# A gated delta-rule chain beside dense projections: the chain's output products are given out one by one behind a projection's product

## The chip, the cores and the metric

One NeuronCore of a Trainium2 chip runs the whole program. The metric is the device time of one execution in microseconds (us); the time of a kernel is the median of its runs.

## The reference

One layer of a streaming encoder for 2048 prompt frames and 32 sample frames of width 1024: a wide input projection, then two branches on the same normalised rows (banded softmax attention, and a gated delta rule with 8 heads of width 64), each gated and projected, merged, projected again and layer-normalised. What matters here is the delta rule, which runs over blocks of 64 frames in order:

```
def step(s, blk_in):
    q_c, k_c, u_c, w_c, gc_c, qk_c = blk_in
    v_new = u_c - einsum('bhld,bhde->bhle', w_c, s)
    o_c = einsum(q_c * exp(gc_c), s) + einsum('bhij,bhje->bhie', qk_c, v_new)
    k_dec = k_c * exp(g_last - gc_c)
    s = s * exp(g_last) + einsum('bhld,bhle->bhde', k_dec, v_new)
    return s, o_c
s_final, o = lax.scan(step, s0, (qb, kb, u, w, gc, qk))
```

The state s of one step needs the one before it; the output o_c is needed by nothing in the scan.

## The kernel before

The prompt is worked in two halves of 1024 frames (the second also carries the 32 sample frames). In each half TensorE runs the input projection as jobs: a job multiplies one 128-column block of weights with all rows, and to keep precision with float16 operands it does so in three products, hi x whi, hi x wlo and lo x whi, of 128x512 or 128x272 (in the order: `pj<-hi,whi` and so on, each with its own weight load `LDWEIGHTS whi` or `LDWEIGHTS wlo`). Meanwhile the delta rule of the heads whose projections are done is prepared (`system`, `solve`, `inverse`, `side`) and then run (`chain`). After these, attention, the branch projections, the merge and the output projection follow, on the same engines.

Nothing here is ordered by a compiler. The code is a set of generators ("streams"). A small planner, `Flow`, keeps a clock for each stream and a busy time for each engine, runs the stream with the earliest clock until it yields, and records its instructions on their engines in that order. `Engine.price` is the planner's cost of an instruction, `Mark` an event that streams may wait for, `Gate` a count of buffers. The engines then run their own queues in the recorded order and wait for each other by semaphores. The helper that records every instruction has one line, L267, so most rows of the profile carry it.

`chain` is one stream in each half. Two heads (a head pair) lie on the 128 partitions as a block-diagonal operand. It runs units of one or two head pairs in turn: a *single* unit has one product of each kind in a step, a *joint* unit two ("lanes"). A half has a single unit, three joint units and a single unit of 8 steps each, and the second half two joint steps of the sample more. A step has these products, all 128x64 in float32:

- `x<-state,k_bd`: keys with the state; VectorE then makes `r`
- `x<-r,u_bd`: the solved system with r; VectorE then makes `vn`, the new values
- `o<-state,q_bd`: the first output product, into bank o, which starts the sum
- `x<-vn,kd_bd`: the state's increment; VectorE then makes the next `state` from it and `faded`, which GpSimd makes (`fade`)
- `o<-vn,qk_bd`: the second output product, which ends the sum in bank o; ScalarE then copies it to `v_t`

The four that read `x` or feed it are the chain; the two into `o` are the outputs. Before, `outputs` records its products at once, right behind those of u_bd and of kd_bd, and puts the stream's clock back so that the planner does not count them in the chain's own time:

```
t = flow.cur.clock
for i, m in enumerate(ms_):
    PE.matmul(os_[i], m, x[:, i], start=not last, stop=last)
flow.cur.clock = t
```

Of the kernel before, what the change touches and what calls it, by code (L numbers as in the profile page):

```python
# [11 lines left out]
F32 = mybir.dt.float32  # L12
# [32 lines left out]


NQK = 4

NPAR, NSIDE = 4, 3
HEAD, TAIL = [2, 3], [6, 5]  # L50
# [28 lines left out]
class Stream:  # L79
    def __init__(self, gen, clock):  # L80
        self.gen, self.clock, self.last = gen, clock, None
# [75 lines left out]
class Flow:  # L157
# [2 lines left out]


    def __init__(self):
        self.heap, self.n, self.busy = [], 0, {}
        self.cur = Stream(None, 0.0)

    def push(self, s, later=0.0):
# [27 lines left out]
    def spend(self, key, cost):  # L194
# [6 lines left out]
        self.busy[key] = s.clock = t  # L201
        s.last = key


    def transfer(self, queue, size):

        start = max(self.cur.clock + 0.2, self.busy.get(queue, 0.0)) + 0.5
        self.busy[queue] = start

        end = max(start + 0.6, self.busy.get("DMA", 0.0)) + size / 360e3  # L210
        self.busy["DMA"] = end
        return end + MARGIN
# [13 lines left out]
class Engine:  # L226
# [36 lines left out]
    def __getattr__(self, name):  # L263
        f = getattr(self.eng, name)

        def call(*a, **k):
            r = f(*a, **k)  # L267
            self.flow.spend(self.key, self.price(name, a, k))
            return r

        setattr(self, name, call)
        return call
# [3 lines left out]
def trunk(ctx: ExitStack, tc: tile.TileContext, x_p, x_s, cache_k, cache_v, st_conv, st_gdn,  # L276
# [4 lines left out]
    flow = Flow()  # L281
    V = Engine(flow, nc.vector, "V")
    S = Engine(flow, nc.scalar, "S")
    G = Engine(flow, nc.gpsimd, "G")
    PE = Engine(flow, nc.tensor, "PE")
# [22 lines left out]
    def gate(n):  # L308
        return Gate(flow, n)

    def places(n):
        return Places(flow, n)

    def mark():
        return Mark(flow)
# [15 lines left out]
    def pt(tag):  # L331

        return bank_pool[tag].tile([P, 512], F32, tag=tag, bufs=banks[tag], name=tag)
# [506 lines left out]
    def phase_b(half):  # L840
# [4 lines left out]
        last = half == 1  # L845
# [77 lines left out]

        raw_slots, qk_slots, v_slots = gate(2), gate(NQK), gate(2)
        par_slots, side_slots, u_slots, p_slots, vt_slots = (places(n) for n in (NPAR, NSIDE, NSIDE, NSIDE, NSIDE))
# [101 lines left out]
        def job_conv(p, i):  # L1027
# [11 lines left out]
            def finish(b):  # L1039
                k = blocks[p][b]  # L1040
                if i == 0:
                    yield qk_slots
                    k.qk = bp.tile([P, 2, 512], F32, tag="qk", bufs=NQK, name=f"qk{p}{b}")
                if i == 2:
# [336 lines left out]
        xb, ob_ = pt("x"), [pt("o")[:, 0:HD] for _ in range(2)]  # L1381
        left = [len(order)]

        def lanes(ap):
            return ap.rearrange("p (l d) -> p l d", d=HD)

        def outputs(ms_, x, os_, last):

            t = flow.cur.clock
            for i, m in enumerate(ms_):  # L1390
                PE.matmul(os_[i], m, x[:, i], start=not last, stop=last)
            flow.cur.clock = t

        def keep(os_, vcs, end):
            yield
            for i, vc in enumerate(vcs):
                S.copy(out=vc, in_=os_[i])
            for m in end:
                m.done()

        def fade(out, st, by, m):
            G.tensor_tensor(out=out, in0=st, in1=by, op=ALU.mult)
            m.done()
            yield

        def chain(units):
            for ks in units:
                for k in ks:
                    yield k.ready
                a = ks[0]  # L1410
                if a.p is None:
                    steps = [([(a, c), (a, c + 1)], a.sc[:, 1, c:c + 2], a.sc[:, 3, c:c + 2], state_s[:, c:c + 2])
                             for c in range(0, NP, 2)]
                else:
                    some = a.both[:, a.lane:a.lane + len(ks)]
                    steps = [([(k, c) for k in ks], some[:, :, 1, c], some[:, :, 3, c], state[:, a.p:a.p + len(ks)])
                             for c in range(8)]
                for n, (who, by, fading, st) in enumerate(steps):
                    m = len(who)
                    by, fading = (x.unsqueeze(2).to_broadcast([P, m, HD]) for x in (by, fading))  # L1420
                    xs, ys, ds_ = (lanes(xb[:, i * P:i * P + m * HD]) for i in range(3))
                    vcs = [k.v_t[:, c if k.p is None else c % 4 * 2 + c // 4, :] for k, c in who]
                    for i, (k, c) in enumerate(who):
                        PE.matmul(xs[:, i], k.kb[:, c, :], st[:, i], start=True, stop=True)
                    faded, kept = bp.tile([P, 2, HD], F32, tag="st", bufs=1, name="st")[:, 0:m], mark()
                    flow.start(fade(faded, st, fading, kept))
                    yield
                    r = bp.tile([P, 2, HD], F32, tag="r", bufs=1, name="r")
                    for i, (k, c) in enumerate(who):
                        V.scalar_tensor_tensor(out=r[:, i], in0=xs[:, i], scalar=k.negc[:, c:c + 1], in1=vcs[i],  # L1430
                                               op0=ALU.mult, op1=ALU.add)
                    yield
                    for i, (k, c) in enumerate(who):
                        PE.matmul(ys[:, i], k.ub[:, c, :], r[:, i], start=True, stop=True)
                    outputs([k.qb[:, c, :] for k, c in who], st, ob_, False)
                    yield
                    vn = bp.tile([P, 2, HD], F32, tag="vn", bufs=1, name="vn")[:, 0:m]
                    V.tensor_tensor(out=vn, in0=ys, in1=by, op=ALU.mult)
                    yield
                    for i, (k, c) in enumerate(who):  # L1440
                        PE.matmul(ds_[:, i], k.kdb[:, c, :], vn[:, i], start=True, stop=True)
                    outputs([k.qkb[:, c, :] for k, c in who], vn, ob_, True)
                    flow.start(keep(ob_, vcs, [k.out for k in ks] if n == len(steps) - 1 else ()),
                               flow.busy["PE"])
                    yield kept
                    yield
                    V.tensor_tensor(out=st, in0=faded, in1=ds_, op=ALU.add)
                    yield
                for k in ks:
                    yield k.out  # L1450
                for k in ks:
                    par_slots.back(k.par)
                    side_slots.back(k.sn)
                    u_slots.back(k.un)
                    flow.start(tail(k))
# [85 lines left out]
        for g in (zeros(), worker(todo), worker(decays), prep(), local(), solve(), solve()):  # L1541
            flow.start(g)
        flow.start(chain([order[0:1], order[1:3], order[3:5], order[5:7], order[7:8]] + [[sample]] * last))
        return stack, make, done

# [954 lines left out]
    for half in range(2):  # L2500
        stack, make, done = phase_b(half)
        enter(1, half, make)
        flow.run(done)
        stack.close()
        stack_w.close()
        if half:
            wr_pool.append(ctx.enter_context(tc.tile_pool(name="wr0", bufs=1)))
            wr_open.done()
            gp = ctx.enter_context(tc.tile_pool(name="gp", bufs=1, reuse_waits="tile"))
            for gen in (early_g(), early_sg(), early(), load_a(), merge()):  # L2510
                flow.start(gen)
        ap, stack, make, done = phase_a(half)
        enter(0, half, make)
        if half == 0:
            flow.start(build_h(1, ap, 4), flow.cur.clock + AHEAD)
        if half == 0:
            flow.run(done)
            flow.run(l_ready[1][8])
            stack.close()
        else:  # L2520
            for p in range(NP):
                dma(ng_p[2 * p:2 * p + 2].rearrange("h k v -> (h k) v"), state[:, p, :])
                dma(ng_s[2 * p:2 * p + 2].rearrange("h k v -> (h k) v"), state_s[:, p, :])
            flow.start(carries(), flow.cur.clock + 20.0)
            flow.run(done)
            stack.close()
# [53 lines left out]
```

## Time and profile before

| | |
|---|---|
| median of 3 runs | 1965.35 us (1964.91 to 1971.32) |
| the profiled execution | 1972.64 us |
| its span on the core | 1970.6 us |
| TensorE (PE) busy | 1905.6 us, 97% |
| VectorE (DVE) busy | 1397.4 us, 71% |
| ScalarE (ACT) busy | 993.9 us, 50% |
| GpSimd (POOL) busy | 806.9 us, 41% |
| mean granted clock of TensorE | 0.984 |

The span is the time from the first to the last instruction in the trace; the execution's own time has some 2 us around it. The profiled execution is one of the longer ones, 7.3 us over the median. PE is the matmuls, PEld the loads of their weights, which run beside them. Matmuls overlap each other in the records, so the durations of a row of them add up to more than the time that passes.

### The profile page before, as it was taken

How to read it: one execution, taken by the hardware profiler on the slowest of the kernel's cores; microseconds unless marked ns; L12 is line 12 of the kernel's file. 1: busy time of each engine (PE TensorE's matmuls, PEld its weight loads, DVE VectorE, ACT ScalarE, POOL GpSimd, SP SyncE). 2: the span in 40 equal slices, each digit the busy share in tenths (PEclk: the TensorE clock that was granted, in tenths of full speed). 3: DMA queues.
4: the chain of work that ended last, by engine and by line, in shares of the span. 5: the costliest groups of instructions: out<-in, count | busy, mean ns of one | idle time of the engine just before them, and what ended most of it. 6: DMA issues, size and time to landing. Idle time of an engine off the chain costs nothing. (4 is left out here: it accounts for less than half of the span.)

```text
span 1970.6 us, 40977 instructions
## 1 busy us (share of the span) xinstructions
PE 1905.6 (97%) x14514; PEld 1348.8 (68%) x14514; DVE 1397.4 (71%) x4252; ACT 993.9 (50%) x2022; POOL 806.9 (41%) x1161
## 2 busy tenths in 40 slices
PE   8999999999999998999999999999999999999998
PEld 5455676666455556666767768768877667988886
DVE  7689988963278768679987986455556565465797
ACT  6665545443587777565544443355356675321110
POOL 7345436424344345444434432422122232243673
PEclk8999999999999999999999998999999999999999
DMA  3234332333368787223232142477878688896552
GB/s 132 71 89 118 72 105 78 91 87 93 115 156 212 165 183 169 77 79 84 76 94 74 52 126 57 130 207 198 223 180 189 168 199 187 255 332 200 174 189 87
DMA packets 382949, 274.61 MB, mean 139 GB/s; under 512 B 248338, under 2 KB 319358, under 8 KB 382744
## 3 DMA queue, kind: packets, MB, share of 16 engines
q1 hardware_dynamic: 382744, 272.00, 51.3%
q8 instruction: 114, 1.87, 0.4%
q14 instruction: 91, 0.75, 0.1%
HBM read 157.15 MB, written 71.76 MB: 116 GB/s over the span
## 5 line engine op out<-in xcount | busy, mean ns | idle before, releaser
L267 PE MATMUL pj<-hi,whi 128*128 128x512 f16 (+2 forms) x1992 | 643.3, 339 | 13.8 <-ACT part L267 3.1
L267 PE MATMUL pj<-hi,wlo 128*128 128x512 f16 (+2 forms) x1952 | 634.1, 339 | 0.7 <-POOL wlo L267 0.7
L267 PEld LDWEIGHTS <-whi 128*128 128x128 f16 x3984 | 395.9, 101 | 247.5 <-issue 7.2
L267 POOL TENSOR_TENSOR wlo<-wraw,whi 128x256 f16<-128x256 f32 (+1 forms) x392 | 282.2, 742 | 375.2 <-ACT whi L267 308.9
L267 PE MATMUL pj<-lo,whi 128*128 128x512 f16 (+2 forms) x1992 | 435.7, 338 | 0.0
L267 PEld LDWEIGHTS <-wlo 128*128 128x128 f16 x1952 | 198.2, 102 | 130.2 <-issue 10.2
L267 ACT ACTIVATE sb<-sb,mx,unit 128x640 f32<-128x640 f32 (+4 forms) x128 | 108.8, 850 | 95.0 <-DVE mx L267 85.6
L267 POOL TENSOR_TENSOR pu<-sb,pu 128x640 f16<-128x640 f32 (+2 forms) x64 | 81.4, 1273 | 178.3 <-ACT pu L267 140.7
L267 ACT ACTIVATE wraw<-wraw,w_scale 128x1024 f32<-128x1024 f32 (+1 forms) x98 | 111.4, 1137 | 81.2 <-DVE w_scale L267 77.7
L267 ACT CAST whi<-wraw 128x512 f16<-128x512 f32 (+2 forms) x212 | 128.1, 610 | 23.8 <-PE pj L267 20.8
L267 DVE SCALAR_TENSOR_TENSOR acc<-raw,cwT,acc 128x512 f32<-128x512 f32 x144 | 114.0, 792 | 13.9 <-ACT acc L267 12.6
L267 ACT CAST mh<-sf 128x256 fp32r<-128x256 f32 x64 | 25.7, 406 | 159.1 <-PE c L267 78.2
L267 DVE CUSTOM_DVE_ANT_0 sb<-a,bias 128x320 f32<-128x320 f32 (+5 forms) x136 | 66.3, 497 | 48.7 <-PE a L267 43.3
L267 ACT ACTIVATE sig<-pj,w_both 128x512 f32<-128x512 f32 (+2 forms) x84 | 49.2, 586 | 93.9 <-PE pj L267 75.3
L267 DVE SCALAR_TENSOR_TENSOR sys_u<-sys_p,sys_u 128x20 f32<-128x20 f32 (+11 forms) x408 | 93.3, 271 | 1.2
L267 POOL TENSOR_TENSOR ml<-sf,mh 128x256 fp32r<-128x256 f32 x60 | 59.7, 997 | 79.1 <-PE c L267 53.1
L267 POOL TENSOR_TENSOR st<-state,sc 128x128 f32<-128x128 f32 (+1 forms) x80 | 31.1, 388 | 148.4 <-DVE state L267 129.4
L267 PE MATMUL b<-ghi,whi 128*128 128x256 f32 (+1 forms) x320 | 89.4, 312 | 0.1
L267 DVE TENSOR_TENSOR sys_t<-sys_u,sys_p 128x60 f32<-128x60 f32 (+17 forms) x323 | 81.9, 254 | 6.0
L267 DVE TENSOR_TENSOR sys_u<-sys_u,sys_t 128x60 f32<-128x60 f32 (+17 forms) x323 | 81.6, 253 | 6.0 <-DVE state L267 0.2
L267 POOL TENSOR_TENSOR w_scale<-w_scale,mhalf 128x1 f32<-128x1 f32 x49 | 32.5, 663 | 124.7 <-DVE w_scale L267 115.3
L267 ACT CAST pu<-sb 128x640 f16<-128x640 f32 (+4 forms) x128 | 81.7, 649 | 0.5
(390 smaller groups left out, 4197.2 us busy)
## 6 DMA issues: line engine op xcount, KB each, us to landing
wraw<-in_w_in SPq DMA_DIRECT2D x192, 256.0 KB
sf<-sig SPq DMA_DIRECT2D x112, 128.0 KB
sig<-sig SPq DMA_DIRECT2D x44, 256.0 KB
sg<-sig SPq DMA_DIRECT2D x37, 256.0 KB
sig<-sg SPq DMA_DIRECT2D x37, 256.0 KB
sys_p<-sol_p SPq DMA_DIRECT2D x68, 128.0 KB
x<-in_x_p SPq DMA_DIRECT2D x16, 512.0 KB
xt<-in_x_p SPq DMA_DIRECT2D x16, 512.0 KB
```

The costliest lines, as they stand in the source:

```text
L267: r = f(*a, **k)
```

## The change

The planner gets a flag, `flow.wide`: whether the last product recorded on TensorE has a float32 weight operand. A generator, `flow.apart()`, yields up to three times (`TRIES`) while the flag is set, each time until 0.05 us (`GAP`) behind TensorE's busy time, so that another stream may record a product first. In `chain` the first of each kind of product asks `apart` before it is recorded, and the second lane's follows at once. The outputs become a stream of their own, started 0.15 us behind TensorE's busy time, in which every product asks `apart`. Since they can now be recorded later than the step that made them, marks keep the order: `taken` (the copies out of bank o are recorded) before the next first output product, `first` (the first output products are recorded) before the second ones and before the state is overwritten. The copies out of bank o, a stream of their own before (`keep`), are recorded at the end of the same stream. The fade is started one yield later.

```
+TRIES, GAP = 3, 0.05
...
+    def apart(self):
+        for _ in range(TRIES):
+            if not self.wide:
+                return
+            yield max(self.cur.clock, self.busy["PE"]) + GAP
...
+            if self.key == "PE":
+                self.flow.wide = a[1].dtype == F32
...
-        def outputs(ms_, x, os_, last):
-            t = flow.cur.clock
+        def outputs(ms_, x, os_, go, gone, vcs=None, end=()):
+            yield go
             for i, m in enumerate(ms_):
-                PE.matmul(os_[i], m, x[:, i], start=not last, stop=last)
-            flow.cur.clock = t
-        def keep(os_, vcs, end):
-            yield
-            for i, vc in enumerate(vcs):
-                S.copy(out=vc, in_=os_[i])
-            for m in end:
-                m.done()
+                yield from flow.apart()
+                PE.matmul(os_[i], m, x[:, i], start=vcs is None, stop=vcs is not None)
+            if vcs is None:
+                gone.done()
+            yield
+            if vcs is not None:
+                for i, vc in enumerate(vcs):
+                    S.copy(out=vc, in_=os_[i])
+                gone.done()
+                for m in end:
+                    m.done()
...
                     for i, (k, c) in enumerate(who):
+                        if not i:
+                            yield from flow.apart()
                         PE.matmul(xs[:, i], k.kb[:, c, :], st[:, i], start=True, stop=True)
+                    first = mark()
+                    yield
...
-                    outputs([k.qb[:, c, :] for k, c in who], st, ob_, False)
+                    flow.start(outputs([k.qb[:, c, :] for k, c in who], st, ob_, taken, first), flow.busy["PE"] + 0.15)
...
-                    outputs([k.qkb[:, c, :] for k, c in who], vn, ob_, True)
-                    flow.start(keep(ob_, vcs, [k.out for k in ks] if n == len(steps) - 1 else ()),
-                               flow.busy["PE"])
+                    taken = mark()
+                    flow.start(outputs([k.qkb[:, c, :] for k, c in who], vn, ob_, first, taken, vcs,
+                                       [k.out for k in ks] if n == len(steps) - 1 else ()), flow.busy["PE"] + 0.15)
+                    yield
                     yield kept
+                    yield first
```

(The products with u_bd and kd_bd get the same two lines on `apart` as that with k_bd.)

What this does to the order of instructions, on TensorE in the first joint step of the first half, from the products with u_bd on (the numbers behind k_bd, u_bd, q_bd, kd_bd and qk_bd are buffers, one for each lane; a float32 product loads its weights itself and has no row for it). Before:

```order
L267 MATMUL x<-r,u_bd_748 128x64
L267 MATMUL x<-r,u_bd_749 128x64
L267 MATMUL o<-state,q_bd_742 128x64
L267 MATMUL o<-state,q_bd_743 128x64
L267 LDWEIGHTS whi
L267 MATMUL pj<-hi_164,whi 128x512
L267 LDWEIGHTS wlo
L267 MATMUL pj<-hi_164,wlo 128x512
```

The same place after:

```order
L275 MATMUL x<-r,u_bd_748 128x64
L275 MATMUL x<-r,u_bd_749 128x64
L275 LDWEIGHTS whi
L275 MATMUL pj<-hi_164,whi 128x512
L275 MATMUL o<-state,q_bd_742 128x64
L275 LDWEIGHTS wlo
L275 MATMUL pj<-hi_164,wlo 128x512
L275 MATMUL o<-state,q_bd_743 128x64
L275 LDWEIGHTS whi
L275 MATMUL pj<-hi_164,whi 128x512
```

Each of the two output products now has a projection's product in front of it and one behind it, where all four float32 products stood in a row.

The second place is the end of the same step on TensorE, from the products with kd_bd to the next step's with k_bd. Before:

```order
L267 MATMUL x<-vn,kd_bd_745 128x64
L267 MATMUL x<-vn,kd_bd_746 128x64
L267 MATMUL o<-vn,qk_bd_738 128x64
L267 MATMUL o<-vn,qk_bd_739 128x64
L267 LDWEIGHTS whi
L267 MATMUL pj<-hi_164,whi 128x512
L267 MATMUL x<-state,k_bd_734 128x64
L267 MATMUL x<-state,k_bd_735 128x64
```

After:

```order
L275 MATMUL x<-vn,kd_bd_745 128x64
L275 MATMUL x<-vn,kd_bd_746 128x64
L275 LDWEIGHTS wlo
L275 MATMUL pj<-hi_164,wlo 128x512
L275 MATMUL o<-vn,qk_bd_738 128x64
L275 LDWEIGHTS whi
L275 MATMUL pj<-hi_164,whi 128x512
L275 MATMUL o<-vn,qk_bd_739 128x64
L275 LDWEIGHTS wlo
L275 MATMUL pj<-hi_164,wlo 128x512
L275 MATMUL x<-state,k_bd_734 128x64
L275 MATMUL x<-state,k_bd_735 128x64
```

Here three projection products stand between kd_bd and the next k_bd, where there was one.

More of the change, by code (lines that the diff above doesn't have):

```diff
@@ L162, in __init__ @@
     def __init__(self):
-        self.heap, self.n, self.busy = [], 0, {}
+        self.heap, self.n, self.busy, self.wide = [], 0, {}, False
         self.cur = Stream(None, 0.0)
@@ L1406, in chain @@
         def chain(units):
+            taken = mark()
+            taken.done()
             for ks in units:
@@ L1433, in chain @@
                     for i, (k, c) in enumerate(who):
+                        if not i:
+                            yield from flow.apart()
                         PE.matmul(ys[:, i], k.ub[:, c, :], r[:, i], start=True, stop=True)
-                    outputs([k.qb[:, c, :] for k, c in who], st, ob_, False)
+                    flow.start(outputs([k.qb[:, c, :] for k, c in who], st, ob_, taken, first), flow.busy["PE"] + 0.15)
                     yield
@@ L1440, in chain @@
                     for i, (k, c) in enumerate(who):
+                        if not i:
+                            yield from flow.apart()
                         PE.matmul(ds_[:, i], k.kdb[:, c, :], vn[:, i], start=True, stop=True)
-                    outputs([k.qkb[:, c, :] for k, c in who], vn, ob_, True)
-                    flow.start(keep(ob_, vcs, [k.out for k in ks] if n == len(steps) - 1 else ()),
-                               flow.busy["PE"])
+                    taken = mark()
+                    flow.start(outputs([k.qkb[:, c, :] for k, c in who], vn, ob_, first, taken, vcs,
+                                       [k.out for k in ks] if n == len(steps) - 1 else ()), flow.busy["PE"] + 0.15)
+                    yield
                     yield kept
+                    yield first
                     yield
```

## The prediction

> **What bounds the kernel now.** I read the page first: the span, the busy shares, and the chain that ended last.
>
> ```profile
> span 1970.6 us, 40977 instructions
> PE 1905.6 (97%) x14514; PEld 1348.8 (68%) x14514; DVE 1397.4 (71%) x4252; ACT 993.9 (50%) x2022; POOL 806.9 (41%) x1161
> PE pj L267 3%; PE a L267 3%; PE b L267 2%; PE c L267 1%; DVE xt L267 0%; POOLq L2574 0%; DVE fst L267 0%; DVE sl L267 0%; DVE m L267 0%; DVEq L267 0%; POOLq L267 0%
> ```
>
> TensorE is busy 97% of the span and the chain consists of its products, so a shorter row of products on TensorE shortens the run. Busy is not peak: matmuls overlap in the records, so what a product costs has to be read from start to start. The second view is therefore the timeline of TensorE inside a joint step and a single step. Columns: start, time covered, engine, line, product, how many of them. A float32 product shows as two records, so x4 is one pair of lanes and x2 one lane.
>
> ```profile
> 360.19 0.38 PE L267 MATMUL pj<-hi,wlo 128*128 128x512 f16 x1
> 360.40 0.38 PE L267 MATMUL pj<-hi,whi 128*128 128x512 f16 x1
> 360.62 0.55 PE L267 MATMUL x<-vn,kd_bd 128*128 128x64 f32 x4
> 361.01 0.61 PE L267 MATMUL o<-vn,qk_bd 128*128 128x64 f32 x4
> 361.46 0.38 PE L267 MATMUL pj<-hi,wlo 128*128 128x512 f16 x1
> 361.67 0.55 PE L267 MATMUL x<-state,k_bd 128*128 128x64 f32 x4
> 362.06 0.38 PE L267 MATMUL pj<-hi,whi 128*128 128x512 f16 x1
> ...
> 459.06 0.33 PE L267 MATMUL x<-state,k_bd 128*128 128x64 f32 x2
> 459.23 0.38 PE L267 MATMUL pj<-hi,whi 128*128 128x512 f16 x1
> ...
> 460.05 0.39 PE L267 MATMUL o<-state,q_bd 128*128 128x64 f32 x2
> 460.27 0.38 PE L267 MATMUL pj<-hi,wlo 128*128 128x512 f16 x1
> ```
>
> A projection's product takes 0.21 to 0.22 us to the next start (360.19, 360.40, 360.62). The same pair of float32 products takes 0.39 us behind a projection's product (360.62 to 361.01; also 361.67 to 362.06) and 0.45 us behind other float32 products (361.01 to 361.46). One lane alone: 0.17 behind a projection's product (459.06 to 459.23), 0.22 behind float32 (460.05 to 460.27). So each float32 group that gets a projection's product in front of it saves 0.05 to 0.06 us, whether it holds one product or two. The projection's product behind the group pays nothing: 361.46 to 361.67 and 362.06 onward are the usual steps.
>
> The weight loads (PEld) show why:
>
> ```profile
> 354.97 0.63 PEld L267 LDWEIGHTS x<-vn,kd_bd 128*128 128x128 f32 x4
> 355.52 0.53 PEld L267 LDWEIGHTS o<-vn,qk_bd 128*128 128x128 f32 x4
> ...
> 355.18 0.55 PE L267 MATMUL x<-vn,kd_bd 128*128 128x64 f32 x4
> 355.57 0.61 PE L267 MATMUL o<-vn,qk_bd 128*128 128x64 f32 x4
> ```
>
> Behind a projection's product the first load starts 0.21 us ahead of its matmul (354.97 to 355.18), beside the 512 columns in flight. Behind a float32 product, it starts 0.05 us ahead (355.52 to 355.57): the product in front streams 64 columns and is over before the load is.
>
> **The change part by part.** *How many groups move.* The rows of the state tiles give the counts:
>
> ```profile
> L267 PE MATMUL o<-vn,qk_bd x264: 274/275/422, 196.5 to 1251.4; 128*128 128x64 f32 x132
> L267 PE MATMUL o<-state,q_bd x256: 274/275/421, 195.4 to 1243.2; 128*128 128x64 f32 x128
> L267 PE MATMUL o<-state_s,q_bd x8: 275/275/276, 1246.4 to 1250.4; 128*128 128x64 f32 x8
> L267 DVE TENSOR_TENSOR vn<-x,sc x82: 208/283/293, 196.0 to 1250.2; 128x128 f32<-128x128 f32 x50, 128x64 f32<-128x64 f32 x32
> ```
>
> There are 82 steps: 50 joint (two lanes) and 32 single, so 132 products of each of the two output kinds. In the order before, all 264 stand behind a float32 product. In the order after, I count 262 of them each behind a projection's product; two of the qk kind are left behind float32. Of the inner chain products, the first with u_bd goes from 78 to 82 such places and the first with kd_bd from 76 to 82; with k_bd it stays at 79. That is 262 + 4 + 6 = 272 groups. At 0.055 us (the middle of 0.05 and 0.06) this is **-15.0 us**; by the two ends -13.6 and -16.3. Step by step it is the same: a joint step's output products fall from 2 x 0.45 to 4 x 0.17, -0.22, times 50 = -11.0; a single step's from 2 x 0.22 to 2 x 0.17, -0.10, times 32 = -3.2; the ten inner groups add -0.6: -14.8 from rounded rows.
>
> The Trainium skill, TensorE: Matmul & The Clock Gate, section LDWEIGHTS (loading the stationary operand), prices a load at columns / 1.2 ns, whatever the element's width: about 107 ns for 128 columns. The trace puts 0.45 / 4 = 0.11 between float32 records, so they agree on what sets that pace; as an estimate, hiding a load of 107 ns where 56 ns were hidden would make the sum 272 x 0.051 = 13.9 us in place of 15.0.
>
> *The k_bd load.* In 271.15 to 272.69 below, k_bd has a projection's product in front and still takes 0.44, since its state was ready too late for the load to run ahead.
>
> ```profile
> 271.58 0.61 PE L267 MATMUL o<-vn,qk_bd 128*128 128x64 f32 x4
> 272.03 0.38 PE L267 MATMUL pj<-lo,whi 128*128 128x512 f16 x1
> 272.25 0.61 PE L267 MATMUL x<-state,k_bd 128*128 128x64 f32 x4
> 272.69 0.38 PE L267 MATMUL pj<-lo,whi 128*128 128x512 f16 x1
> ```
>
> In the order after, mostly more products stand between kd_bd and the next k_bd. If that helps, it is worth up to 0.05 for each such step, of which I count 16 in the timeline: 0 to -0.8. I take -0.4.
>
> *The early branch products.* Of their 512 triples, 40 more use bank b in place of pj. The first of a run costs more than the next:
>
> ```profile
> 1301.42 0.36 PE L267 MATMUL b<-ghi,whi 128*128 128x256 f32 x1
> 1301.62 0.28 PE L267 MATMUL b<-ghi,wlo 128*128 128x256 f32 x1
> 1301.73 0.28 PE L267 MATMUL b<-ghi,whi 128*128 128x256 f32 x1
> ```
>
> 0.20 against 0.11; nine more such runs start behind a projection's product, +0.8 if all are new, 0 if the runs are as many as before. I take +0.4.
>
> *New waits.* The output products with q_bd now wait for a mark that the last step's copies out of bank o set. Those copies were given out a whole step earlier, and so I cost the wait at nothing; if a copy is late, everything behind it on TensorE waits, by the longest such wait below. The state's update on VectorE now also needs the q_bd products to be done; in both orders shown they stand ahead of kd_bd, for which it waits anyway: nothing. ScalarE's copies out of o come later by the products put in between (some 0.4 to 0.8 us a step). ScalarE already stands 101.1 us there:
>
> ```profile
> ACT v_t L267 <- PE o L267: 101.1, 57, 5.0
> PEld x L267 <- DVE r L267: 14.0, 37, 2.4
> PE x L267 <- DVE r L267: 2.6, 3, 1.9
> ```
>
> Behind them on ScalarE are the splits of weights into whi and TensorE's bank evacuations; at 50% busy it has room. The fade on GpSimd moves behind k_bd's mark by nothing that the order shows. No DMA is added or removed; SP's queue keeps its kinds and amounts, shifted by some rows. I price the whole reshuffle at zero with an uncertainty: it moves waits, and a wait on TensorE can cost more than its length:
>
> ```profile
> 1018.52 0.38 PE L267 MATMUL pj<-hi,whi 128*128 128x512 f16 x1
> 1020.76 0.66 PE L267 MATMUL x<-r,u_bd 128*128 128x64 f32 x4 [1.86 <-DVE r L267]
> ...
> 1019.00:1022.10 3.10, 1.33 (x11) 1.20 (x11) 3.03 (x13) 0.58 (x3) 1.18 (x4) 1.00 0.12 20
> 1022.10:1028.90 6.80, 6.80 (x28) 5.24 (x28) 4.02 (x22) 0.65 (x3) 0.40 (x1) 0.50 0.41 107
> 1195.00:1199.50 4.50, 4.50 (x87) 3.96 (x87) 3.73 (x17) 0.87 (x3) 0.17 (x1) 1.00 0.02 4
> 1199.60:1209.80 10.20, 10.20 (x43) 8.25 (x42) 5.10 (x20) 4.00 (x10) 3.36 (x6) 0.50 0.12 41
> ```
>
> (Windows: stretch, its length, then PE, PEld, DVE, ACT, POOL busy, the granted clock, DMA share, GB/s.) After u_bd waited 2.0 us beyond a product's usual step, the clock was granted at 0.50 for 6.8 us, which costs half of it: 2.0 + 3.4 = 5.4 us. The stretch from 1199.6 costs 5.1 us, with TensorE busy all of the 4.50 us ahead of it.
>
> *Sum.* -15.0 - 0.4 + 0.4 = **-15.0 us**. The profiled execution took 1972.64 us around its span of 1970.6, so it becomes 1957.6. It lies 7.3 us above the median of the runs, 1965.35; against that median the forecast is **1950.4 us**, -0.76%. A measurement of this kernel tells about 0.3% from no change, 5.9 us.
>
> **The rivals.** *VectorE takes the gain back (about 1962).* Where chains start, VectorE is nearly full:
>
> ```profile
> 190.00:290.00 100.00, 96.79 (x799) 64.89 (x799) 94.18 (x358) 55.22 (x117) 44.83 (x80) 1.00 0.39 100
> 940.00:1010.00 70.00, 68.00 (x594) 50.94 (x593) 67.14 (x241) 37.90 (x82) 30.03 (x58) 1.00 0.29 76
> ```
>
> For: 94.18 of 100 and 67.14 of 70. Against: the first window holds 8 single and 8 joint steps, 8 x 0.10 + 8 x 0.22 = 2.6 us, and 100 - 2.6 is still over 94.18; the second holds 8 single steps, 0.8 us of the 2.9 that VectorE has free. Two new waits like that at 1018.74, 10.8 us, would leave -4.2: about 1961, no change to be told.
>
> *Slower.* The same mechanism, more often: TensorE reaches u_bd sooner after k_bd, r is not there, and the half clock follows. It decides from four such waits: 21.6 - 15.0 = +6.6; with five, 1965.35 + 12.0 = 1977. Against: the matmuls' waits on r come to 2.6 us in 3, with one that long (the weight loads' 14.0 in 37 lie mostly beside a product in flight), and the order has about as many products between k_bd and u_bd as before.
>
> *The half clock recedes (about 1942).* The stretch from 1199.6 follows busy time in which joint steps run, with float32 products that spend half of their 0.11 us on loads; the change takes them apart there and fills the array better. If it and the one at 1022.1 go, 5.1 + 3.4 = 8.5 us more: 1950.4 - 8.5 = 1941.9. Against: the next order can have its own. The page named above, Part 1, says the clock follows how busy TensorE has been in windows of 3.4 us; the lengths here, 6.8 and 10.2, are multiples of that, and the second stretch shows that idle time is not needed.
>
> *The place makes no difference (1965).* If loads were hidden behind whatever product is in front, nothing would be won. The 0.45 against 0.39 of the same shapes speak against it. The same page, Part 2, Step-by-step, has the next tile's weights load while this one's matmul runs, without a word on how long that matmul is; taken so, it is this rival, and the rows say otherwise.
>
> **How the numbers follow.** Forecast 0.65; half clock recedes 0.17; gain taken back by VectorE's waits or never there 0.12 (0.02 of it the last rival); slower 0.06. So faster 0.65 + 0.17 = 0.82, same 0.12, slower 0.06. The range has the receding half clock at its low end, 1942, and two new waits at its high end, 1950.4 + 10.8 = 1961; the forecast's own range, by 0.05 and 0.06 a group and the two small terms, is 1948 to 1953.
>
> **What the profile after would show.** Right: o<-state,q_bd and o<-vn,qk_bd spaced 0.17 to the projection's product behind them, their first load beside the projection's product in front, start to start of projections unchanged at 0.216. VectorE's, ScalarE's and GpSimd's busy times unchanged. Wrong: spacing of 0.22 in those places; or the spacing as forecast and the time given back in waits of x<-r and x<-vn, or in more stretches at 0.50, or at bank evacuations where TensorE now comes sooner.

## The result and the profile after

The changed kernel takes 1947.7 us (median of 4 runs, 1947.63 to 1948.82), against 1968.34 for the kernel before (4 runs, 1964.91 to 1975.17): a ratio of 0.9895 with a 95% interval of 0.9872 to 0.9919. That is 20.6 us less. The profiled execution took 1947.72 us.

The page after, first the lines that answer to those before:

```profile
span 1945.9 us, 40936 instructions
PE 1876.0 (96%) x14514; PEld 1341.5 (69%) x14514; DVE 1388.9 (71%) x4252; ACT 990.4 (51%) x2022; POOL 807.2 (41%) x1161
PE pj L275 3%; PE a L275 3%; PE b L275 2%; PE c L275 1%; DVE xt L275 0%; POOLq L2597 0%; DVE fst L275 0%; DVE sl L275 0%; DVE m L275 0%; POOLq L275 0%
```

The other engines have the instructions they had; VectorE's busy time is 8.5 us less and ScalarE's 3.5, and why was not followed up. The chain that ended last is the same products of TensorE. Then TensorE's timeline in a joint step, from u_bd on:

```profile
272.84 0.55 PE L275 MATMUL x<-r,u_bd 128*128 128x64 f32 x4
273.23 0.38 PE L275 MATMUL pj<-hi,wlo 128*128 128x512 f16 x1
273.44 0.33 PE L275 MATMUL o<-state,q_bd 128*128 128x64 f32 x2
273.61 0.38 PE L275 MATMUL pj<-hi,whi 128*128 128x512 f16 x1
...
274.95 0.38 PE L275 MATMUL pj<-hi,wlo 128*128 128x512 f16 x1
275.17 0.33 PE L275 MATMUL o<-vn,qk_bd 128*128 128x64 f32 x2
275.34 0.38 PE L275 MATMUL pj<-hi,whi 128*128 128x512 f16 x1
275.55 0.33 PE L275 MATMUL o<-vn,qk_bd 128*128 128x64 f32 x2
275.72 0.38 PE L275 MATMUL pj<-hi,wlo 128*128 128x512 f16 x1
```

And two rows of its weight loads (PEld) in the same step:

```profile
273.23 0.41 PEld L275 LDWEIGHTS o<-state,q_bd 128*128 128x128 f32 x2
...
274.96 0.41 PEld L275 LDWEIGHTS o<-vn,qk_bd 128*128 128x128 f32 x2
```

Each output product takes 0.17 us (273.44 to 273.61, 275.17 to 275.34, 275.55 to 275.72), and its first load now starts 0.21 us ahead of it, beside the projection's product (273.23 to 273.44). That is the price forecast, and it holds over the whole trace: the median start to start of a single 128x64 float32 product is 0.168 us in the 505 places behind a float16 product and 0.223 in the 155 behind float32; in the kernel before it is 0.168 in 233 places and 0.223 in 427. The waits around the chain (total us, times, longest):

```profile
ACT v_t L275 <- PE o L275: 74.7, 71, 3.4
...
PEld x L275 <- DVE r L275: 18.1, 48, 1.3
...
DVE state L275 <- PE o L275: 6.9, 5, 3.6
...
PE x L275 <- DVE r L275: 4.2, 9, 0.8
```

The loads of u_bd wait for r longer than before in total (18.1 us against 14.0), the longest wait is shorter (1.3 against 2.4). The row of `state` is new: five times VectorE may not overwrite the state yet because a q_bd product still has to read it. By the order of starts on TensorE, 9 of the 132 q_bd products leave behind the kd_bd product of their own lane; before, none did. The third thing that differs is the granted clock. Stretches of the second half's chains, columns as in the prediction; the first three rows are of the kernel before, the last three of the one after:

```profile
1010.00:1120.00 110.00, 107.10 (x966) 85.78 (x964) 89.53 (x305) 50.01 (x122) 44.69 (x83) 0.97 0.26 72
1120.00:1180.00 60.00, 56.96 (x485) 41.28 (x484) 54.43 (x211) 27.21 (x57) 25.77 (x44) 0.94 0.42 116
1180.00:1255.00 75.00, 74.72 (x654) 61.09 (x653) 45.03 (x190) 26.93 (x74) 26.05 (x49) 0.93 0.27 76
```

```profile
1010.00:1120.00 110.00, 108.55 (x959) 88.08 (x958) 94.91 (x347) 55.70 (x133) 46.57 (x89) 0.98 0.28 76
1120.00:1180.00 60.00, 57.68 (x552) 44.86 (x551) 54.85 (x228) 22.82 (x51) 23.75 (x42) 1.00 0.44 120
1180.00:1255.00 75.00, 74.88 (x663) 59.78 (x662) 30.48 (x128) 31.11 (x78) 32.27 (x56) 1.00 0.35 101
```

0.97, 0.94 and 0.93 became 0.98, 1.00 and 1.00; over the whole span the clock rose from 0.984 to 0.994. (The stretches are the same times, not quite the same work: the last q_bd product of the chains starts at 1243.2 us before and at 1223.1 after.)

To say how much each of these three is worth, I split every trace's span in the same way. For each product on TensorE I take the time from its start to the next product's start. Products are sorted by kind (operand type and columns, with the type of the product in front and behind); the median of each kind in the trace of before is its price. The *base* is the sum of these prices over all products. What a start-to-start time has over its price is a *wait* where the clock is granted in full, and *half-clock loss* in the stretches granted 0.50. Some 10.5 us at the two ends are left out. How a product that is cut by the edge of a stretch is sorted, and which kinds are told apart, moves single numbers by 2 to 3 us, so differences of that size are not read. Each row splits one profiled execution, that of before 1972.64 us long.

| kernel | groups behind a projection's product | median us | base | waits | half-clock loss |
|---|---|---|---|---|---|
| before | 233 | 1965.35 to 1969.45, by session | 1845.5 | 85.4 | 29.3 |
| after | 505 | 1947.7 | 1831.1 | 94.8 | 9.5 |
| after, profiled again | 505 | 1947.85 | 1831.1 | 91.3 | 13.2 |

From profile to profile the base fell by 14.4 us, waits rose by 6 to 9, and the half-clock loss fell by 16 to 20. The last of these is too large for a typical execution, since that of before is one of the longer ones. The granted clock of every execution is on record, and (1 - clock) x span estimates what the clock took: on average 25 us over 78 executions of before (in the sessions of the experiments) and 14 us over 9 of the changed kernel, so about 11 us less.

### The profile page after: what moved, and what is told of

Read it like the earlier page. It is cut to its first block, busy times and chain, and to the rows that moved or that the text cites. A ratio compares the mean times of both kernels' runs of the same rounds, so it can differ in the third digit from the quotient of the medians.

```text
span 1945.9 us, 40936 instructions
## 1 busy us (share of the span) xinstructions
PE 1876.0 (96%) x14514; PEld 1341.5 (69%) x14514; DVE 1388.9 (71%) x4252; ACT 990.4 (51%) x2022; POOL 807.2 (41%) x1161
## 5 line engine op out<-in xcount | busy, mean ns | idle before, releaser
L275 PEld LDWEIGHTS <-whi 128*128 128x128 f16 x3984 | 404.5, 103 | 229.2 <-issue 2.7
L275 PE MATMUL pj<-lo,whi 128*128 128x512 f16 (+2 forms) x1992 | 445.8, 337 | 0.0
L275 PEld LDWEIGHTS <-wlo 128*128 128x128 f16 x1952 | 202.3, 104 | 115.7 <-issue 10.1
L275 PE MATMUL b<-ghi,whi 128*128 128x256 f32 (+1 forms) x360 | 99.8, 310 | 1.7 <-DVE cr L275 1.3
L275 PE MATMUL b<-ghi,wlo 128*128 128x256 f32 (+1 forms) x360 | 89.8, 282 | 0.0
L275 DVE SCALAR_TENSOR_TENSOR sg<-sg,b 128x512 f32<-128x512 f32 (+2 forms) x53 | 32.3, 610 | 78.5 <-PE b L275 73.8
L275 PEld LDWEIGHTS <-pt 128*128 128x128 f16 x1680 | 65.8, 98 | 25.7 <-issue 7.0
```

## The experiments

**The changed kernel again**, beside the kernels of the next three experiments.

> The changed kernel once more, beside the kernels it is compared with. Both theories: ratio to the kernel before 0.987 to 0.992, as measured (0.9895), with a profile that has about 20 us of the span at half clock, where the profile of before had about 60.

Measured: 1947.85 us, ratio 0.9882 (0.9858 to 0.9907), 31 us of the span at half clock in the profile (about 20 were expected) against 64 before. The time repeats.

**The place alone, from the changed kernel.** The plan is that of the changed kernel; at the place where the plan has an output product only its cost is booked, and the product itself is given to TensorE right behind u_bd or kd_bd. All other rows of the five engines keep their order.

```
+        def put_now(ms_, x, os_, last):
+            for i, m in enumerate(ms_):
+                PE.eng.matmul(os_[i], m, x[:, i], start=not last, stop=last)
...
+                if there:
+                    flow.wide = True
+                    flow.spend("PE", PE.price("matmul", (os_[i], m, x[:, i]), {}))
+                else:
                     PE.matmul(os_[i], m, x[:, i], ...)
...
+                    if early:
+                        put_now([k.qb[:, c, :] for k, c in who], st, ob_, False)
```

> The changed kernel's plan, with the output products put back right behind the chain's products in TensorE's queue and nothing else moved on any engine (all other rows of all five engines stand in the same order). Float32 chain and output groups behind a projection's product: 246, against 505 in the changed kernel and 233 before. Theory 1 (the place of each group is worth 0.056 us): 259 x 0.056 = 14.5 us over the changed kernel, about 1962, ratio to before 0.997. Theory 2 (the new plan has fewer waits and less half clock, the place itself matters little): the time of the changed kernel, 1948, ratio 0.990.

Measured: 1961.59 us, ratio 0.9964 (0.9946 to 0.9983), 13.7 us over the changed kernel. TensorE's timeline:

```profile
272.33 0.55 PE L275 MATMUL x<-r,u_bd 128*128 128x64 f32 x4
272.73 0.61 PE L1400 MATMUL o<-state,q_bd 128*128 128x64 f32 x4
273.17 0.38 PE L275 MATMUL pj<-hi,wlo 128*128 128x512 f16 x1
```

The outputs take 0.44 again. Base 1845.5, that of the kernel before; waits 90.6 and half-clock loss 15.3, like those of the changed kernel profiled again. With the plan held still, the place is worth what theory 1 says; theory 2 falls for this term.

This kernel has the places of before and the plan of after, and it is still 6.2 us under the kernel before (1967.75 in that session). So about 14 of the 20 us come from the place and the rest from the new plan. By the same estimate as above that rest is half clock: (1 - clock) x span is 16 us on average here against 25 before, and what is left of the span is 1944 here against 1943.

**The place alone, from the kernel before.** The plan is that of before, and the output products are held back, with ScalarE's copies out of bank o behind them.

```
+            if self.key == "PE" and a[1].dtype == F16:
+                self.flow.held_one()          # the next output product leaves here
...
+                    flow.flush("qk", "copy")  # before vn is overwritten
                     V.tensor_tensor(out=vn, in0=ys, in1=by, op=ALU.mult)
...
+                    flow.flush("q")           # before state is overwritten
                     V.tensor_tensor(out=st, in0=faded, in1=ds_, op=ALU.add)
```

> The plan of before, with nothing moved but the output products: each is held back until a projection's float16 product has been recorded and then leaves behind it (ScalarE's copies out of bank o follow them). Groups behind a projection's product: 413, against 233 before; fewer than in the changed kernel since chain products then often stand right behind an output product. Theory 1: 180 x 0.056 = 10.1 us under before, about 1957, ratio 0.995. Theory 2: the time of before, 1967, ratio 1.000.

Measured: 1985.55 us, ratio 1.0072 (1.0047 to 1.0097): slower, which neither theory had. The base did fall, by 9.9 us to 1835.6, as theory 1 has it. But waits rose to 106.1. The timeline and, behind it, the waits (total us, times, longest) name the place:

```profile
273.42 0.33 PE L1410 MATMUL o<-state,q_bd 128*128 128x64 f32 x2
273.75 0.66 PE L282 MATMUL x<-vn,kd_bd 128*128 128x64 f32 x4
274.25 0.38 PE L282 MATMUL pj<-lo,whi 128*128 128x512 f16 x1
274.46 0.33 PE L1410 MATMUL o<-state,q_bd 128*128 128x64 f32 x2
275.24 0.66 PE L282 MATMUL x<-state,k_bd 128*128 128x64 f32 x4 [0.45 <-DVE state L282]
```

```profile
DVE state L282 <- PE o L1410: 24.6, 22, 2.2
...
PE x L282 <- DVE state L282: 9.3, 21, 0.8
```

The second lane's q_bd product is now behind kd_bd. VectorE may overwrite the state only when it is done, and waited 24.6 us for that where before it did not show such a wait at all; the next k_bd then waits for the state (TensorE 9.3 us against 1.1 before, its loads 16.6 against 6.5). The place won its 9.9 us in the base and lost more in the chain. Here 27 of the 132 q_bd products leave behind their lane's kd_bd. In the changed kernel, whose plan was made with the outputs in their new places, it is 9, and VectorE waits 6.9 us for them.

**More of it: every chain product asks, the second lane's too.**

```
-                        if not i:
-                            yield from flow.apart()
+                        yield from flow.apart()
```

> The changed kernel with every chain product asking for a place behind a projection's product, the second lane's too: 655 groups against 505. Theory 1: 150 x 0.056 = 8.4 us under the changed kernel, about 1939, ratio to before 0.985, unless the chain, which now has three more projection products in a joint step, is late somewhere. Theory 2: no order to be told, within 5 us of the changed kernel on either side.

Measured: 1959.39 us, ratio 0.9941 (0.9921 to 0.9961): 11.5 over the changed kernel, where theory 1 had 8.4 under and theory 2 at most 5 either way: both missed the time. The base fell by 7.7 to 1823.4, near the 8.4 of theory 1, but waits are 108.2 and the half-clock loss 21.4:

```profile
PE x L275 <- DVE r L275: 9.7, 12, 2.1
PE c L275 <- DVE ob L275: 7.8, 4, 3.4
PE pj L275 <- ACT part L275: 6.0, 1, 6.0
```

u_bd waits more for r (9.7 us against 4.2). The 6.0 us for one bank evacuation by ScalarE lie in another stage, where the new plan has ScalarE and VectorE busy with other work.

**New plans without the change, and with it.** If places explain the base, what sets the waits and the half clock? One number of the planner was changed in both kernels. It moves instructions on all engines and leaves the places of the groups.

```
-HOP_PE, HOP, HOP_SAME = 0.1, 0.2, 0.12
+HOP_PE, HOP, HOP_SAME = 0.12, 0.2, 0.12      # h1; in h2: 0.1, 0.22, 0.12
```

> The kernel before with one number of the planner changed (HOP_PE 0.12 in place of 0.1), which reorders all engines and leaves the places of the outputs as they were: 227 groups behind a projection's product, against 233. By places alone 6 x 0.056 = 0.3 us more than before. Theory 1 (what the change won beyond its places, some 5 us, is the luck of a new plan): 1963 to 1973, with waits at full clock and half-clock time that differ from those of before by several us either way. Theory 2 (the outputs' own stream keeps the clock up): half-clock time of about 60 us again, 1967 within 3.

> As the last one, with HOP 0.22 in place of 0.2: 229 groups. Theory 1: 1963 to 1973 and another mix of waits and half clock. Theory 2: 1967 within 3.

> The changed kernel with HOP_PE 0.12: 509 groups against 505. Places alone: 0.2 us under the changed kernel. Theory 1: 1944 to 1956, since the changed kernel's own plan was a good one. Theory 2: half-clock time of 20 to 35 us as in the changed kernel, 1948 within 3.

> The changed kernel with HOP 0.22: 506 groups. Theory 1: 1944 to 1956. Theory 2: 1948 within 3. Both: the mean of these two lies some 15 us under the mean of the two made from before, as 281 groups x 0.056 = 15.7 us.

| kernel | groups | median us | ratio to before | base | waits | half-clock loss |
|---|---|---|---|---|---|---|
| before, h1 | 227 | 1965.4 | 0.9971 (0.9952 to 0.9991) | 1844.9 | 87.0 | 21.3 |
| before, h2 | 229 | 1965.63 | 0.9972 (0.9954 to 0.9991) | 1847.2 | 84.1 | 22.5 |
| after, h1 | 509 | 1969.97 | 0.9997 (0.998 to 1.0015) | 1830.1 | 102.7 | 25.4 |
| after, h2 | 506 | 1962.19 | 0.9948 (0.9925 to 0.997) | 1832.3 | 96.8 | 23.4 |

Theory 2 falls here: with the change and another plan, the half-clock loss is 23 to 25 us, as without it. Theory 1 had the direction and too small a span: 1969.97 and 1962.19 are outside its 1944 to 1956, and the two means lie 0.6 us apart the wrong way, not 15. What does hold is the base: 1830 to 1832 in three plans with the change, 1845 to 1847 in three without. But waits are 91 to 103 with it and 84 to 87 without. TensorE's own waits for r and its loads' waits are part of that, here first of h1 and then of h2, both with the change:

```profile
PEld x L275 <- DVE r L275: 28.7, 53, 1.7
...
PE x L275 <- DVE r L275: 11.3, 16, 1.3
```

```profile
PEld x L275 <- DVE r L275: 30.3, 53, 2.3
...
PE x L275 <- DVE r L275: 12.3, 16, 1.8
```

TensorE's own waits for r are 11.3 and 12.3 us, against 4.2 in the changed kernel and 2.6, 1.3 and 5.5 in before, its h1 and its h2; those of the loads are 28.7 and 30.3, against 18.1 and 14.0, 14.2 and 18.0. In each of the two pairs the waits are up by about as much as the base is down: 15.7 and 14.8 us in h1, 12.7 and 14.9 in h2.

**Is it the planner's prices?** The planner prices a float32 product of 64 columns at 0.213 us, wherever it stands. A joint step of ten is 2.13; in the trace before it took 0.39 + 2 x 0.84 = 2.07, and after 3 x 0.39 + 4 x 0.17 = 1.85. So TensorE would run ahead of the plan and come too early for r. The prices were set to the traces:

```
             if a[1].dtype == F16:
-                return max(n / 2400.0, m / 4800.0)
+                return max(n / 2400.0, m / 4800.0) + 0.0026
...
+            if name != "transpose" and n == 64 and m == P:
+                return 0.224 if self.flow.behind else 0.168
```

(`behind` is the flag `wide` as it stood before this product.)

> The changed kernel with the planner's prices of TensorE's products set to what the traces show: a float32 128x64 product 0.168 us behind a projection's product and 0.224 behind float32 (it was 0.213 for both), a float16 product 0.0026 us more. 506 groups, as in the changed kernel. Theory A (in the plans made from the changed kernel u_bd waits more for r since TensorE runs ahead of a plan that prices a joint step's float32 products at 2.13 us where they take 1.85): the waits at u_bd fall from 7 to 17 us to the 3 to 7 us of the plans made from before, and the time is 1938 to 1950. Theory B (each new plan has waits of its own, whatever its prices): waits at u_bd and half-clock time anywhere in the spans seen so far, 1948 to 1970.

> The same prices with HOP_PE 0.12 (the kernel without the prices took 1970): 506 groups. Theory A: 1940 to 1955, waits at u_bd under 8 us in place of 14.5. Theory B: 1948 to 1970.

> The same prices with HOP 0.22 (the kernel without the prices took 1962): 509 groups. Theory A: 1940 to 1955, waits at u_bd under 8 us in place of 16.6. Theory B: 1948 to 1970.

> The same prices, and every chain product asks for a place behind a projection's product, the second lane's too: 654 groups (the kernel without the prices took 1959). Places alone: 149 x 0.056 = 8.3 us under a kernel with 505. Theory A: under the changed kernel, 1932 to 1945. Theory B: 1940 to 1962.

| kernel | groups | median us | ratio to before | base | waits | half-clock loss |
|---|---|---|---|---|---|---|
| prices | 506 | 1971.65 | 1.0014 (0.9994 to 1.0034) | 1830.8 | 102.6 | 30.1 |
| prices, h1 | 506 | 1970.18 | 1.0011 (0.9995 to 1.0027) | 1830.0 | 108.9 | 21.6 |
| prices, h2 | 509 | 1966.3 | 0.998 (0.9962 to 0.9997) | 1832.3 | 105.5 | 16.1 |
| prices, every product asks | 654 | 1965.26 | 0.9995 (0.9972 to 1.0018) | 1823.6 | 101.1 | 26.3 |

Theory A falls as a way to win time: no plan with truer prices is under 1965. TensorE's waits for r are 5.9 to 6.5 us in the three: about half of what h1 and h2 had, over the 4.2 of the changed kernel. So the waits at u_bd did fall under the 8 us of theory A, but all waits together did not: 102.6 to 108.9 us in these three, 96.8 and 102.7 in h2 and h1 without the prices. The longest others in the first of the four are spread over other stages:

```profile
PE x L277 <- DVE r L277: 5.9, 10, 1.6
PE d L277 <- DVE qk_bd L277: 5.6, 5, 2.1
PE b L277 <- DVE sg L277: 5.0, 2, 3.2
PE a L277 <- ACT mh L277: 4.8, 1, 4.8
```

Theory B had waits of no fixed place, and these have none; its upper bound, 1970, was passed by 1.7 and 0.2, and its 1962 for the last kernel by 3.3. No experiment beat the changed kernel.

## Why the prediction was right, and where not

The forecast was 1950.4 us in a range of 1942 to 1961, and 1947.7 came out. Point by point:

- **272 groups at 0.055, -15.0 us.** Right. The spacing is 0.17 and the base fell by 14.4 us. With the plan held still the same 13.7 to 14.4 come out (the kernel with the outputs put back), and in the two kernels with 413 and 655 groups the base followed the count (9.9 of 10.1 us, 7.7 of 8.4). The Trainium skill, TensorE: Matmul & The Clock Gate, section LDWEIGHTS (loading the stationary operand), would by its 107 ns for 128 columns have made 13.9, as an estimate; the measured 14.4 lies between that and 15.0 and does not tell the two apart.
- **k_bd's load and the early branch products, -0.4 and +0.4.** Not to be seen apart from the rest.
- **The reshuffle, priced at zero.** This term was mis-sized, in two parts that happened to cancel some of each other: waits +6 to +9 us and half-clock loss -16 to -20 between the profiles, about -11 between typical executions. The wait part was, in part, the rival on VectorE: u_bd's loads wait 18.1 us for r against 14.0, and with other plans 28.7 and 30.3. The argument against it was that VectorE has room left in each window. (Its first window holds 6 joint steps and not 8, by VectorE's `vn` rows, so 2.1 us and not 2.6, which changes nothing there.) It did not see this; a likely reason, not shown, is that u_bd waits for one late instruction in VectorE's queue and not for its total. The half-clock part was the rival that the half clock recedes. The two stretches named for it are gone, but others came.
- **That the net came out near the forecast** is in part the luck of this plan: the place gave about 14 us, and a plan with less half clock the rest. Measured over three plans of each kind, the medians with the change are 1947.7, 1970.0 and 1962.2, without it 1968.3, 1965.4 and 1965.6: means of 1960.0 and 1966.4. Three more plans with the change, made with other prices, took 1971.7, 1970.2 and 1966.3. The forecast's 0.82 for faster was too sure for a change that makes every later instruction move.
- **New waits costed at nothing.** For bank o and ScalarE that held: the loads of the output products wait 1.0 us in all for the copies out of it, and ScalarE's idle time before its copies is 74.7 us in 71 waits, against 101.1 in 57. For the state's overwriting it did not quite hold. The prediction read two places in the order, where q_bd stands ahead of kd_bd; 9 of 132 do not, and VectorE stood 6.9 us for them, 3.6 us once. TensorE's own waits for the state rose only from 1.1 to 2.4 us, its loads' from 6.5 to 8.1. The kernel with held-back outputs shows the price where it happens more often: 24.6 us of VectorE's time.

What stays open: why the waits at full clock rise in every plan with the change. Waits for r and, in attention, for `ob` are part of them; the planner's prices are not their cause, or not alone. A rival stands: in h1 and h2 the waits took back about all that the base gave, as they would if another engine set the pace of the chains there and TensorE only reached its next wait sooner. Only in the changed kernel's plan was the place taken away with nothing else moved; put into the plan of before, it lost more than it won. So that the place is worth its 14 us in other plans too is not shown. Nor is it settled what starts a half-clock stretch.

## What to carry to other kernels

Read a small product's price from start to start, by what stands in front of it: here the same float32 product takes 0.17 us behind a projection's product and 0.22 behind another float32 product, and counting such places in the order gave what the row of products gained to within 1 us. Whether the run gains as much is a second question: with the plan held still 13.7 us came through, and in two other plans the waits rose by as much as the products fell. Where a planner reorders everything after an edit, one run of one plan tells as much of the plan as of the edit; change a number that should not matter in both kernels, or hold the plan still and move the products alone.

## What the runs showed of the hardware

A half-clock stretch can follow a short wait. In the changed kernel, u_bd started 1.06 us behind a projection's product, 0.84 over the usual step, and the clock was granted at about half shortly after for 3.4 us (the timeline, then the window):

```profile
1072.24 0.38 PE L275 MATMUL pj<-hi,wlo 128*128 128x512 f16 x1
1073.30 0.66 PE L275 MATMUL x<-r,u_bd 128*128 128x64 f32 x4 [0.68 <-DVE r L275]
```

```profile
1075.20:1078.60 3.40, 3.40 (x15) 3.05 (x16) 2.62 (x11) 0.10 (x1) 2.96 (x4) 0.51 0.00 0
```

In the second profile of the same kernel the same pair stands at 1072.8 and 1075.1. But waits of 0.79 and 0.77 us for u_bd at 337.5 and 953.3 had no half clock behind them, so this is a sequence and not shown to be the cause. Over all the traces 24 to 71 us of an execution's span ran at half clock and cost some 10 to 33 us, beside the 14 us of the places; the runs of the kernel before alone span 1959 to 1978 us.
